# Parked S5 matrices loaded back transfer by transfer, small mixer weights split one stage earlier, and a margin before the step transposes, in a two-block fp32 kernel

## The chip, the cores and the metric

The kernel runs on 1 core of one Trainium2 chip. The metric is device microseconds of one execution, taken as the median of several runs. Engines are named as in the profile: PE is TensorE matmul, PEld its weight loads, DVE is VectorE, ACT is ScalarE, POOL is GpSimd, SP is SyncE, which computes nothing and issues the DMAs of one queue in program order.

## What is computed

The reference runs two blocks on 256 tokens of width 1024, in float32. The first is a hybrid attention block with a mixture of 32 experts. The second, which the change touches, is two layers of feed-forward, mixer, feed-forward:

```python
def second_block(x, ...):
    h = x
    for i in range(DEPTH_2):
        f = swiglu(rmsnorm(h, ffn1_pre_g[i]), ffn1_w_gate[i], ffn1_w_up[i], ffn1_w_down[i])
        h = h + 0.5 * rmsnorm(f, ffn1_post_g[i])
        m = mixer(rmsnorm(h, mix_pre_g[i]), w_in[i], ...)
        h = h + rmsnorm(m, mix_post_g[i])
        f = swiglu(rmsnorm(h, ffn2_pre_g[i]), ffn2_w_gate[i], ffn2_w_up[i], ffn2_w_down[i])
        h = h + 0.5 * rmsnorm(f, ffn2_post_g[i])
    return h

def mixer(u, ...):
    proj = u @ w_in
    z, xbc, dt_raw, u5, g_a, g_b = jnp.split(proj, SPLITS, axis=-1)
    y_a = ssd_branch(z, xbc, dt_raw, ...) @ w_branch_a
    y_b = s5_branch(u5, ...) @ w_branch_b
    return (jax.nn.sigmoid(g_a) * y_a + jax.nn.sigmoid(g_b) * y_b) @ w_out
```

`ssd_branch` needs the step `dt = softplus(dt_raw + bias)` and its running sums. `s5_branch` is a complex linear recurrence over 64 groups; the kernel runs it in blocks of time with matrices that depend on the weights alone.

## The kernel before

Products of float32 are made as three matmuls of two rounded halves (`mm3`: high by high, high by low, low by high). So each weight unit, 1 MB loaded by SP into one of three buffers (`raw`, `NRAW = 3`), is split in two halves of 1024 columns: ACT casts the high part (`whi`), POOL or DVE subtracts to get the low part (`wlo`), and PE uses both. Four halves exist at a time; a cast waits for PE to be done with the half four before, and a load waits for the second subtraction of the unit three before (`drop`, `load`). A half is 24 matmuls of 256 columns.

The order of instructions on every engine is written out at build time by a small planner. `Clocks` and `Engine` hold a planned time for each engine from a cost for each instruction; side work runs as generators (`Thread`), and `stir`, called after every six matmuls of a unit, takes the next step of each thread whose planned time `ready` has come (within `EARLY` = 0.7 us of PE's planned clock). A thread that yields a float waits so many planned us of PE's clock (`step`). The planner counts a 256-column matmul as 256 x 0.00042 = 0.1075 us and a 256 KB load as 0.73 us behind those before it (`spread`).

The feed-forward stage (`ffn`) streams 33 units: 22 of gate and up, 11 of down. The mixer starts with the boundary (normalization and the first product), four units `u` for the S5 input, the small product for the step (`dps`, 24 matmuls with the split weights `dw`), then the units of `PLAN`, eight of `z` first.

Three side works matter here. `s5_pre` computed the S5 matrices during the expert stage and parked them in DRAM (`ld`, `gd`, `kd`, `ed`). `s5_build` loads them back during a feed-forward stage: for layer 0 in the first one, for layer 1 in the second of layer 0; `mixer` finishes it before the first `z`. For each half it loads `LT` and `BT` (eight transfers of 256 KB that fill 64 rows each, written with a source whose outer dimension is 4) and `toep` (eight of 64 KB from `kd`), and multiplies `LT` and `BT` on DVE (`cmul`, six operations). Then it loads `G` and `E` (eight of 512 KB over 128 rows). The waits between are `GAP`. `ssd_steps` makes `dt` and the sums from `dps` and has PE transpose them. `small_weights` in the mixer scales the convolution weights `cw` and splits `dtw` into `dw`.

All work is recorded at L155, the helper of `Engine`, so rows are told apart by their tiles: `ffn_`, `bnd_`, `u_`, `z_`, `x_`, `dt_`, `s5b_` (build), `s5i_` (run), `ssd_`. `p` is a ring of working tiles.

Of the kernel before, what the change touches and what calls it, by code (L numbers as in the profile page):

```python
# [10 lines left out]
F32 = mybir.dt.float32  # L11
F32R = mybir.dt.float32r
# [3 lines left out]
P = 128  # L16
T = 256
KD = 8
# [3 lines left out]
def dram_ap(t, offset, dims):  # L22
    return bass.AP(tensor=t.tensor, offset=t.offset + offset, ap=[list(d) for d in dims])
# [155 lines left out]
class Core:  # L179
# [4 lines left out]
    KEEP = ("raw", "whi", "wlo", "ident", "causal", "ones_d", "ones_g", "eps", "one", "one32", "junk", "id16", "s5_r4", "vecs")  # L184
    MID = ("iota", "four", "group", "upper", "ones", "mod", "adaA", "rw", "rb")
    NRAW = 3
    GAP = 20.0, 10.0, 25.0, 12.0
    LENT = ()
    pages, stop = None, 1 << 30
    lab = "k"  # L190
# [62 lines left out]
    def vec(self, name):  # L253
        off, n = self.voff[name]
        return self.vecs[:, off:off + n]
# [186 lines left out]
    def step(self, th):  # L442
        c, lab = self.nc, self.lab
        n, c.end, self.stepping, self.lab = c.count, 0.0, True, th.lab
        th.step()
        th.lab, self.lab, self.stepping = self.lab, lab, False
        if c.count > n:
            th.ready = c.end
        if isinstance(th.wait, float):
            th.ready = c.tensor.clock + th.wait  # L450
        if th.done:
            self.threads.remove(th)
        return c.count > n or th.done
# [146 lines left out]
class Block2(Core):  # L600
# [219 lines left out]
    def s5_pre(self, l):  # L820
# [113 lines left out]
        for hf in range(2):  # L934
            self.lab = "s5b"
            G = t8([P, 2, H, 4, 16])
            pp = slice(hf * H, hf * H + H)
            cr, nci = G0[:, 0, pp], G0[:, 1, pp]
            tmp = t4([P, 2, 2, H, 16])
            for k in range(4):  # L940
# [66 lines left out]
    def s5_build(self, l, res):  # L1007

        nc, a = self.nc, self.a
        NP, H = 32, 16  # L1010
        made = self.s5_made[l]
        ld, kd = made["ld"], made["kd"]
        self.lab = "s5b"
        toep, win = [], []
        for hf in range(2):
            yield self.GAP[hf]
            yield from self.need(p4=8)
            self.lab = "s5b"
            tp = self.p4([P, H, 64])
            LT = self.p4([P, H, 64]), self.p4([P, H, 64])  # L1020
            BT = self.p4([P, H, 64]), self.p4([P, H, 64])
            for g in range(2):
                rows = slice(g * 64, g * 64 + 64)
                for ri in range(2):
                    nc.sync.dma_start(LT[ri][rows], dram_ap(ld, ((ri * 2 + g) * 4 * NP + hf * H) * 64, [[NP * 64, 4], [0, 16], [1, H * 64]]))
                    nc.sync.dma_start(BT[ri][rows], dram_ap(a["s5_bt"], (((l * 2 + ri) * 2 + g) * 16 * NP + hf * H) * 64,
                                                            [[0, 4], [NP * 64, 16], [1, H * 64]]))
                for j in range(4):
                    r0 = g * 64 + j * 16
                    nc.sync.dma_start(tp[r0:r0 + 16], dram_ap(kd, hf * H * 32 * 112 + g * 16 * 112 + (3 - j) * 16,  # L1030
                                                              [[112, 16], [32 * 112, H], [1, 64]]))
            yield self.GAP[2]
            self.lab = "s5b"
            wr, wi, tmp = (self.p4([P, H, 64]) for _ in range(3))
            for _ in self.cmul(wr, wi, LT[0], LT[1], BT[0], BT[1], wi, tmp):
                yield
            self.give(p4=3 if hf else 5)
            toep.append(tp)
            win.append((wr, wi))
        yield from self.need(p4=8)  # L1040
        self.lab = "s5b"
        G = [[self.p4([P, H, 4, 16]) for _ in range(2)] for _ in range(2)]
        E = [[self.p4([P, H, 64]) for _ in range(2)] for _ in range(2)]
        for hf in range(2):
            for ri in range(2):
                half = slice(ri * 1024, ri * 1024 + 1024)
                nc.sync.dma_start(E[hf][ri].rearrange("p h m -> p (h m)"), made["ed"][hf, :, half])
                nc.sync.dma_start(G[hf][ri].rearrange("p h k c -> p (h k c)"), made["gd"][hf, :, half])
            yield self.GAP[3]
        res.update(win=win, toep=toep, G=G, E=E, r4=made["r4"])  # L1050


# [139 lines left out]

    def ssd_steps(self, l, dps, r, res):

        nc, a, v = self.nc, self.a, self.v
        self.lab = "dt"
        hvt = self.t([32, 2], "hvt")
        nc.gpsimd.dma_start(hvt, a["hvec"][l])  # L1200
        y, e, u, w_, dt, adt, ac = (self.p1()[:32] for _ in range(7))
        v.tensor_mul(y, dps, r[:32])
        self.give(ps=1)
# [19 lines left out]
        for c in range(2):  # L1223
            cc = slice(c * P, c * P + P)
            v.tensor_tensor_scan(ac[:, cc], self.one32, adt[:, cc], 0.0, op0=ALU.mult, op1=ALU.add)
        yield 2
        yield from self.need(ps=1)
        self.lab = "dt"
        acd = self.scratch([32, T], "acd")
# [149 lines left out]

    def mixer(self, l, h, banks, build, s5):
        nc, a = self.nc, self.a
        v, q = self.v, self.q
        gpre = self.vec(f"mpre{l}")
        lead, xu, rstd = self.boundary(h, banks, self.vec(f"f1post{l}"), gpre, "u")
        self.lab = "u5"
        cw = self.t([P, 24, 5], "cw")
        nc.sync.dma_start(cw, a["conv2"][l])
        dtw = self.p1([P, KD, 32])  # L1390
        nc.sync.dma_start(dtw, a["wdt"][l])
        dw = self.p1([P, KD, 32], F32R), self.p1([P, KD, 32], F32R)
        ud = self.scratch([1024, T], "ud")

        def ev_u5(grp, ps):
# [30 lines left out]
        r = rstd()  # L1426
# [2 lines left out]
        sc = self.defer(scale)  # L1429
        self.budget = self.BM  # L1430

        def small_weights():
            v.tensor_scalar_mul(cw, cw, 0.5)
            nc.scalar.copy(dw[0], dtw)
            yield
            v.tensor_sub(dw[1], dtw, dw[0].bitcast(F32))
        for g in (2, 3):
            pg = self.bank()
            self.unit_mm(("u", g), xu, pg)
            self.defer(lambda g=g, pg=pg: ev_u5(g, pg))  # L1440
            if g == 2:
                sw = self.defer(small_weights)
        self.finish(sw)
        self.roomy, self.busy, self.seen = False, 0, 0
        dps = self.bank()[:32, :T]
        for k in range(KD):
# [2 lines left out]
        self.settle()  # L1449
        s5t = self.spawn(self.s5_run(s5, ud, s5))  # L1450
        sd = {}
        self.spawn(self.ssd_steps(l, dps, r, sd))
        self.finish(sc)
        xg, zg, gat = FM([None] * 6), FM([None] * 4), FM([None] * 4)

# [111 lines left out]
        for grp in range(8):  # L1567
            self.lab = "ba"
            ps = self.bank()
            for i in range(2):  # L1570
                w = [z.rearrange("p (k c) -> p k c", k=KD) for z in self.half(("ba", grp))]
# [35 lines left out]
    def block2(self, h, layers=2, first=None):  # L1607
        self.scale_gains(layers)
        banks, g = None, None
        s5, build = first or self.s5_start(0)  # L1610
        for l in range(layers):
            vec = lambda name: self.vec(f"{name}{l}")
            self.budget = self.BF if l else self.B0
            acc = self.ffn(l, h, banks, g, vec("f1pre"))
            acc = self.mixer(l, h, acc, build, s5)
            self.budget = self.BF
            if l + 1 < layers:
                s5, build = self.s5_start(l + 1)
            banks, g = self.ffn(l, h, acc, vec("mpost"), vec("f2pre")), vec("f2post")
        self.close(h, banks, g)  # L1620
# [1376 lines left out]
```

## Time and profile before

| | us |
|---|---|
| median of 3 runs | 3071.73 (3071.64 to 3073.94) |
| the profiled execution | 3076.65 |
| its span, first to last instruction | 3074.4 |
| PE busy | 2668.1 (87%) |
| DVE busy | 1689.6 (55%) |
| POOL busy | 1442.4 (47%) |
| mean granted clock of PE | 0.95 |

The profiled execution took 4.9 us more than the median. Of its time the first block takes about 1279 us, then come, by the first PE work of each stage: feed-forward 1 of layer 0 (1279 to 1517), its mixer (to 1975), feed-forward 2 (to 2210), feed-forward 1 of layer 1 (to 2410), its mixer (to 2871) and feed-forward 2 (to the end). A row of the trace gives a start and a length in us, or for a group the busy time; brackets hold the idle time of that engine before it and what ended it. A granted clock of 1.00 is 2.4 GHz and 0.50 is 1.2 GHz. Rows of the DMA give the share of 16 DMA engines that was busy and the rate.

### The profile page before, as it was taken

How to read it: one execution, taken by the hardware profiler on the slowest of the kernel's cores; microseconds unless marked ns; L12 is line 12 of the kernel's file. 1: busy time of each engine (PE TensorE's matmuls, PEld its weight loads, DVE VectorE, ACT ScalarE, POOL GpSimd, SP SyncE). 2: the span in 40 equal slices, each digit the busy share in tenths (PEclk: the TensorE clock that was granted, in tenths of full speed). 3: DMA queues.
4: the chain of work that ended last, by engine and by line, in shares of the span. 5: the costliest groups of instructions: out<-in, count | busy, mean ns of one | idle time of the engine just before them, and what ended most of it. 6: DMA issues, size and time to landing. Idle time of an engine off the chain costs nothing.

```text
span 3074.4 us, 55096 instructions
## 1 busy us (share of the span) xinstructions
PE 2668.1 (87%) x22727; PEld 2062.3 (67%) x22727; DVE 1689.6 (55%) x2657; ACT 1020.0 (33%) x1516; POOL 1442.4 (47%) x733
## 2 busy tenths in 40 slices
PE   5768988889889888877989888977999889998998
PEld 4655333333333333577979888977999889888998
DVE  8995242333433211355577888655554685886644
ACT  4562100001000000233445554433444445544444
POOL 7651000000000000256756666756788657766786
PEclk9778999999999999998999999988999999999999
DMA  7526999999999999655545434455555445444453
GB/s 285 191 86 262 420 420 394 420 420 417 418 419 417 414 421 420 255 171 185 195 144 168 157 138 140 162 171 185 192 181 190 157 122 179 151 151 138 162 185 120
DMA packets 146540, 755.09 MB, mean 246 GB/s; under 512 B 47264, under 2 KB 51824, under 8 KB 59760
## 3 DMA queue, kind: packets, MB, share of 16 engines
q1 hardware_dynamic: 140672, 729.30, 62.6%
q0 software_dynamic: 5472, 21.71, 1.9%
q8 instruction: 183, 3.00, 0.4%
q14 instruction: 69, 0.57, 0.1%
q10 hardware_dynamic: 144, 0.52, 0.0%
HBM read 736.50 MB, written 14.97 MB: 244 GB/s over the span
## 4 chain that ended last, share of the span: by engine, by line
PE 36%; DVE 10%; issue 4%; DMA 3%; ACT 2%; POOL 2%; SPq 1%; ACTq 0%; DVEq 0%; POOLq 0%
PE ffn_ps L155 18%; PE x_ps L155 3%; PE ba_ps L155 3%; DVE ssd_p L155 3%; PE g_ps L155 2%; DMA s5b_p<-s_bt 2%; PE glu_ps L155 2%; PE bnd_ps L155 2%; PE z_ps L155 2%; POOL ffn_wlo L155 2%; PE wo_ps L155 1%; DVE x_p L155 1%; PE ssd_ps L155 1%; DVE u_p L155 1%; SPq L155 1%
## 5 line engine op out<-in xcount | busy, mean ns | idle before, releaser
L155 POOL TENSOR_TENSOR ffn_wlo<-ffn_raw,ffn_whi 128x1024 fp32r<-128x1024 f32 x227 | 569.9, 2537 | 178.4 <-ACT ffn_whi L155 172.7
L155 PE MATMUL ffn_ps<-bnd_p,ffn_whi 128*128 128x256 f32 x2560 | 469.2, 285 | 28.8 <-ACT ffn_whi L155 28.8
L155 PEld LDWEIGHTS ffn_ps<-bnd_p,ffn_whi 128*128 128x128 f32 x2560 | 404.5, 194 | 29.6 <-ACT ffn_whi L155 29.6
L155 PE MATMUL ffn_ps<-bnd_p,ffn_wlo 128*128 128x256 f32 x1280 | 366.4, 286 | 13.7 <-POOL ffn_wlo L155 13.7
L155 ACT CAST ffn_whi<-ffn_raw 128x1024 fp32r<-128x1024 f32 x232 | 240.3, 1046 | 259.4 <-PE ffn_ps L155 174.0
L155 PE MATMUL down_ps<-up_place,tr_p 128*32 128x512 f32 (+1 forms) x2048 | 244.0, 614 | 82.1 <-DMA up_place<-edn 82.1
L155 DVE TENSOR_TENSOR ffn_p<-ffn_p,ffn_p 128x256 f32<-128x256 f32 (+1 forms) x184 | 260.9, 1420 | 91.8 <-ACT ffn_p L155 91.4
L155 PE MATMUL ffn_ps<-ffn_p,ffn_whi 128*128 128x256 f32 x1408 | 258.9, 286 | 29.5 <-ACT ffn_whi L155 28.1
L155 PEld LDWEIGHTS ffn_ps<-bnd_p,ffn_wlo 128*128 128x128 f32 x1280 | 248.8, 194 | 15.9 <-POOL ffn_wlo L155 15.9
L155 PE MATMUL up_ps<-down_place,prep_p 128*32 128x512 f32 (+1 forms) x1920 | 224.8, 596 | 21.4 <-DMA down_place<-eup 21.3
L155 PEld LDWEIGHTS ffn_ps<-ffn_p,ffn_whi 128*128 128x128 f32 x1408 | 222.5, 194 | 30.1 <-ACT ffn_whi L155 28.5
L155 PE MATMUL up_ps<-up_place,prep_p 128*32 128x512 f32 (+1 forms) x2048 | 230.2, 595 | 8.3 <-DMA up_place<-eup 8.2
L155 PEld LDWEIGHTS down_ps<-up_place,tr_p 128*32 128x32 f32 x2048 | 67.8, 112 | 244.6 <-issue 200.5
L155 DVE TENSOR_SCALAR glu_p<-up_ps 128x512 f32<-128x512 f32 x64 | 44.1, 691 | 311.7 <-PE up_ps L155 311.7
L155 PE MATMUL ffn_ps<-ffn_p,ffn_wlo 128*128 128x256 f32 x704 | 201.0, 286 | 0.9 <-DVE ffn_wlo L155 0.9
L155 DVE TENSOR_TENSOR ffn_p<-ffn_ps,ffn_p 128x512 f32<-128x512 f32 x80 | 55.1, 689 | 208.6 <-PE ffn_ps L155 208.4
L155 PEld LDWEIGHTS up_ps<-up_place,prep_p 128*32 128x32 f32 x2048 | 61.8, 109 | 150.3 <-issue 129.1
L155 DVE COPY scat_p<-down_ps 128x512 f32<-128x512 f32 x16 | 11.1, 691 | 245.7 <-PE down_ps L155 245.7
L155 PEld LDWEIGHTS up_ps<-down_place,prep_p 128*32 128x32 f32 x1920 | 57.3, 109 | 129.2 <-issue 125.5
L155 PEld LDWEIGHTS ffn_ps<-ffn_p,ffn_wlo 128*128 128x128 f32 x704 | 136.7, 194 | 1.5 <-DVE ffn_wlo L155 1.5
L155 POOL DMA_DIRECT2D ed<-s5b_raw x4 | 2.1, 538 | 262.8 <-DVE s5b_raw L155 262.8
L155 POOL TENSOR_TENSOR scat_wlo<-scat_raw,scat_whi 128x1024 fp32r<-128x1024 f32 x2 | 4.7, 2364 | 251.1 <-ACT scat_whi L155 251.1
(832 smaller groups left out, 6547.7 us busy)
## 6 DMA issues: line engine op xcount, KB each, us to landing
up_place<-eup SPq DMA_DIRECT2D x128, 1024.0 KB, 10.9
up_place<-edn SPq DMA_DIRECT2D x128, 1024.0 KB, 13.7
down_place<-eup SPq DMA_DIRECT2D x120, 1024.0 KB, 14.1
ffn_raw<-gu SPq DMA_DIRECT2D x75, 1024.0 KB, 5.0
ffn_raw<-dn SPq DMA_DIRECT2D x40, 1024.0 KB, 4.9
x_raw<-win SPq DMA_DIRECT2D x22, 1024.0 KB, 5.0
z_raw<-win SPq DMA_DIRECT2D x16, 1024.0 KB, 4.9
g_raw<-win SPq DMA_DIRECT2D x10, 1024.0 KB, 5.4
```

Source lines behind the costliest of these rows:

```text
L155: return f(out, *args, **kw)
```

## The change

- `s5_build` no longer issues the loads of a half in one go. It waits `GAP[0]` = 8 planned us, then issues one `LT` and one `BT` at a time with `GAP[1]` = 5 after each pair, four pairs to a half; after the fourth `GAP[2]` = 8 and the multiplication on DVE. The same for the second half. Then `E` (four loads, 5 after each), `toep` (sixteen, `GAP[3]` = 4 after each) and `G` (four, 5 after each). It asks for 7, 7, 4 and 8 tiles of the ring instead of 8, 8 and 8.
- `mixer_small` is a new thread that starts with the feed-forward 1 of each layer. It loads `cw`, `hvt` and `dtw` by SP, waits 40 planned us, and scales and splits them, into tiles of their own. The mixer no longer loads or splits them, and `ssd_steps` no longer loads `hvt` by POOL.
- A thread may yield a negative float: it is then ready that many planned us after its own last operation ends or after PE's planned clock, whichever is later. `ssd_steps` yields -6.0 in place of 2 before the transposes.

```diff
-    GAP = 20.0, 10.0, 25.0, 12.0
+    GAP = 8.0, 5.0, 8.0, 4.0
...
-            th.ready = c.tensor.clock + th.wait
+            th.ready = c.tensor.clock + th.wait if th.wait > 0 else max(c.end, c.tensor.clock) - th.wait
...
+        yield self.GAP[0]
         for hf in range(2):
-            yield self.GAP[hf]
-            yield from self.need(p4=8)
-            self.lab = "s5b"
-            tp = self.p4([P, H, 64])
+            yield from self.need(p4=7)
             LT = self.p4([P, H, 64]), self.p4([P, H, 64])
             BT = self.p4([P, H, 64]), self.p4([P, H, 64])
             for g in range(2):
                 rows = slice(g * 64, g * 64 + 64)
                 for ri in range(2):
+                    self.lab = "s5b"
                     nc.sync.dma_start(LT[ri][rows], dram_ap(ld, ((ri * 2 + g) * 4 * NP + hf * H) * 64, [[NP * 64, 4], [0, 16], [1, H * 64]]))
                     nc.sync.dma_start(BT[ri][rows], dram_ap(a["s5_bt"], (((l * 2 + ri) * 2 + g) * 16 * NP + hf * H) * 64,
                                                             [[0, 4], [NP * 64, 16], [1, H * 64]]))
-                for j in range(4):
-                    r0 = g * 64 + j * 16
-                    nc.sync.dma_start(tp[r0:r0 + 16], dram_ap(kd, hf * H * 32 * 112 + g * 16 * 112 + (3 - j) * 16,
-                                                              [[112, 16], [32 * 112, H], [1, 64]]))
+                    yield self.GAP[1]
             yield self.GAP[2]
...
-        yield from self.need(p4=8)
+        yield from self.need(p4=4)
         self.lab = "s5b"
-        G = [[self.p4([P, H, 4, 16]) for _ in range(2)] for _ in range(2)]
         E = [[self.p4([P, H, 64]) for _ in range(2)] for _ in range(2)]
         for hf in range(2):
             for ri in range(2):
...
+                nc.sync.dma_start(E[hf][ri].rearrange("p h m -> p (h m)"), made["ed"][hf, :, ri * 1024:ri * 1024 + 1024])
+                yield self.GAP[1]
+        yield from self.need(p4=8)
+        self.lab = "s5b"
+        toep = [self.p4([P, H, 64]) for _ in range(2)]
+        for hf in range(2):
+            for g in range(2):
+                for j in range(4):
...
+                    nc.sync.dma_start(toep[hf][r0:r0 + 16], dram_ap(kd, hf * H * 32 * 112 + g * 16 * 112 + (3 - j) * 16,
+                                                                    [[112, 16], [32 * 112, H], [1, 64]]))
+                    yield self.GAP[3]
...
+                nc.sync.dma_start(G[hf][ri].rearrange("p h k c -> p (h k c)"), made["gd"][hf, :, ri * 1024:ri * 1024 + 1024])
+                yield self.GAP[1]
...
-        hvt = self.t([32, 2], "hvt")
-        nc.gpsimd.dma_start(hvt, a["hvec"][l])
...
-        yield 2
+        yield -6.0
         yield from self.need(ps=1)
...
+    def mixer_small(self, l):
+
+        nc, a = self.nc, self.a
+        self.lab = "msm"
+        cw, hvt, dtw = self.t([P, 24, 5], "cw"), self.t([32, 2], "hvt"), self.t([P, KD, 32], "dtw")
+        dw = self.t([P, KD, 32], "dwh", dt=F32R), self.t([P, KD, 32], "dwl", dt=F32R)
+        for t, w in ((cw, "conv2"), (hvt, "hvec"), (dtw, "wdt")):
+            nc.sync.dma_start(t, a[w][l])
+        self.small = cw, dw, hvt
+        yield 40.0
+        self.lab = "msm"
+        self.v.tensor_scalar_mul(cw, cw, 0.5)
+        nc.scalar.copy(dw[0], dtw)
+        yield
+        self.v.tensor_sub(dw[1], dtw, dw[0].bitcast(F32))
...
+            self.early = self.spawn(self.mixer_small(l))
             acc = self.ffn(l, h, banks, g, vec("f1pre"))
```

## Rows read from the trace of the kernel before

**Rows 1.** Stages: length; busy PE, PEld, DVE, ACT, POOL; PEclk, DMA share, GB/s
```profile
1279.00:1516.80 237.80, 200.75 (x1587) 198.51 (x1587) 124.14 (x100) 92.65 (x130) 158.19 (x67) 0.92 0.54 182
1975.50:2209.20 233.70, 196.72 (x1571) 194.30 (x1572) 128.88 (x107) 91.16 (x127) 158.76 (x67) 0.92 0.53 182
2220.00:2410.20 190.20, 189.20 (x1572) 188.81 (x1572) 95.03 (x92) 91.84 (x127) 160.00 (x70) 1.00 0.50 172
1516.80:1975.50 458.70, 411.41 (x3742) 396.96 (x3742) 348.54 (x490) 217.92 (x297) 307.60 (x147) 0.95 0.46 152
```

**Rows 2.** Waits of PE, 1275 to 1525: us in total, times, longest
```profile
PE ffn_ps L155 <- ACT ffn_whi L155: 28.2, 3, 14.4
...
PE ffn_ps L155 <- POOL ffn_wlo L155: 6.3, 4, 1.9
```

**Rows 3.** Timeline of SP's queue, 1270 to 1530: start, length, instruction
```profile
1320.57 0.69 SPq L155 DMA_DIRECT2D s5b_p<-ld  x1
...
1339.12 5.65 SPq L155 DMA_DIRECT2D s5b_p<-kd  x4
1344.89 2.48 SPq L155 DMA_DIRECT2D ffn_raw<-dn  x1
```

**Rows 4.** DMA issues, KB each, median us to landing: 1319.9-1339, 1338.8-1352, 2220-2410.2
```profile
s5b_p<-kd SPq DMA_DIRECT2D x4, 64.0 KB, 15.3
...
s5b_p<-kd SPq DMA_DIRECT2D x4, 64.0 KB, 12.4
...
ffn_raw<-gu SPq DMA_DIRECT2D x18, 1024.0 KB, 5.0
```

**Rows 5.** Short stretches of the first batch, columns as in rows 1
```profile
1342.00:1346.00 4.00, 0.00 (x0) 0.00 (x0) 0.00 (x0) 0.00 (x0) 0.00 (x0) 1.00 0.33 112
...
1350.00:1354.00 4.00, 0.00 (x0) 0.00 (x0) 0.00 (x0) 0.00 (x0) 0.00 (x0) 0.50 1.00 357
```

**Rows 6.** Timelines of SP, ACT, POOL, 2278 to 2300, no parked loads
```profile
2280.50 6.86 SPq L155 DMA_DIRECT2D ffn_raw<-gu  x2
...
2292.63 1.04 ACT L155 CAST ffn_whi<-ffn_raw 128x1024 fp32r<-128x1024 f32 x1
...
2293.75 7.52 POOL L155 TENSOR_TENSOR ffn_wlo<-ffn_raw,ffn_whi 128x1024 fp32r<-128x1024 f32 x3 [1.75 <-ACT ffn_whi L155]
```

**Rows 7.** A stretch at the lower clock, columns as in rows 1
```profile
1383.80:1390.40 6.60, 4.68 (x23) 4.68 (x23) 3.46 (x2) 3.01 (x5) 6.60 (x3) 0.50 0.18 35
```

**Rows 8.** Waits of PE in the mixer of layer 0, 1517 to 1975
```profile
PE dt_ps L155 <- DVE dt_p L155: 7.9, 2, 4.2
...
PE u_ps L155 <- DVE u_p L155: 4.7, 1, 4.7
...
PE u_ps L155 <- ACT u_p L155: 1.6, 1, 1.6
```

**Rows 9.** Chain that ended last, 1545 to 1605: start, length, what
```profile
1557.45 4.42 PE u_ps L155 x22
...
1599.40 3.56 PE z_ps L155 x18
```

**Rows 10.** Timeline of DVE, 1551 to 1600: start, length, instruction
```profile
1552.55 1.61 DVE L155 TENSOR_SCALAR u_cw<-u_cw 128x120 f32<-128x120 f32 x1
1554.08 2.58 DVE L155 TENSOR_TENSOR u_p<-u_p,u_p 128x256 fp32r<-128x256 f32 x1
...
1558.05 0.97 DVE L155 TENSOR_TENSOR u_p<-u_p,u_p 128x256 fp32r<-128x256 f32 x2
...
1567.72 0.67 DVE L155 TENSOR_SCALAR dt_p<-dt_p,dt_hvt 32x256 f32<-32x256 f32 x1 [5.40 <-DMA dt_hvt<-hvec]
1577.39 0.75 DVE L155 TENSOR_TENSOR s5i_p<-s5i_ps,s5b_p 128x256 f32<-128x256 f32 x2 [9.00 <-PE s5i_ps L155]
```

**Rows 11.** Timeline of POOL, 1550 to 1566
```profile
1554.03 2.35 POOL L155 TENSOR_TENSOR u_wlo<-u_raw,u_whi 128x1024 fp32r<-128x1024 f32 x1
```

**Rows 12.** A stretch of the mixer, columns as in rows 1
```profile
1580.00:1600.00 20.00, 12.12 (x139) 11.35 (x139) 19.69 (x28) 7.05 (x9) 10.18 (x6) 0.88 0.24 82
```

More of the change, by code (lines that the diff above doesn't have):

```diff
@@ L1036, in s5_build @@
                 yield
-            self.give(p4=3 if hf else 5)
-            toep.append(tp)
+            self.give(p4=5)
             win.append((wr, wi))
-        yield from self.need(p4=8)
+        yield from self.need(p4=4)
         self.lab = "s5b"
-        G = [[self.p4([P, H, 4, 16]) for _ in range(2)] for _ in range(2)]
         E = [[self.p4([P, H, 64]) for _ in range(2)] for _ in range(2)]
@@ L1045, in s5_build @@
             for ri in range(2):
[L1046 to L1049, printed above, removed]
+                self.lab = "s5b"
+                nc.sync.dma_start(E[hf][ri].rearrange("p h m -> p (h m)"), made["ed"][hf, :, ri * 1024:ri * 1024 + 1024])
+                yield self.GAP[1]
+        yield from self.need(p4=8)
+        self.lab = "s5b"
+        toep = [self.p4([P, H, 64]) for _ in range(2)]
+        for hf in range(2):
+            for g in range(2):
+                for j in range(4):
+                    self.lab = "s5b"
+                    r0 = g * 64 + j * 16
+                    nc.sync.dma_start(toep[hf][r0:r0 + 16], dram_ap(kd, hf * H * 32 * 112 + g * 16 * 112 + (3 - j) * 16,
+                                                                    [[112, 16], [32 * 112, H], [1, 64]]))
+                    yield self.GAP[3]
+        self.lab = "s5b"
+        G = [[self.p4([P, H, 4, 16]) for _ in range(2)] for _ in range(2)]
+        for hf in range(2):
+            for ri in range(2):
+                self.lab = "s5b"
+                nc.sync.dma_start(G[hf][ri].rearrange("p h k c -> p (h k c)"), made["gd"][hf, :, ri * 1024:ri * 1024 + 1024])
+                yield self.GAP[1]
         res.update(win=win, toep=toep, G=G, E=E, r4=made["r4"])
@@ L1191, in s5_run, with ssd_steps @@
         self.give(p4=2)
-    def ssd_steps(self, l, dps, r, res):
+    def ssd_steps(self, hvt, dps, r, res):
         nc, a, v = self.nc, self.a, self.v
         self.lab = "dt"
-        hvt = self.t([32, 2], "hvt")
-        nc.gpsimd.dma_start(hvt, a["hvec"][l])
         y, e, u, w_, dt, adt, ac = (self.p1()[:32] for _ in range(7))
@@ L1387, in mixer @@
         self.lab = "u5"
[L1388 to L1392, printed above, removed]
+        self.finish(self.early)
+        cw, dw, hvt = self.small
         ud = self.scratch([1024, T], "ud")
@@ L1430, in mixer @@
         self.budget = self.BM
[L1432 to L1436, printed above, removed]
         for g in (2, 3):
@@ L1440, in mixer @@
             self.defer(lambda g=g, pg=pg: ev_u5(g, pg))
-            if g == 2:
-                sw = self.defer(small_weights)
-        self.finish(sw)
         self.roomy, self.busy, self.seen = False, 0, 0
@@ L1451, in mixer @@
         sd = {}
-        self.spawn(self.ssd_steps(l, dps, r, sd))
+        self.spawn(self.ssd_steps(hvt, dps, r, sd))
         self.finish(sc)
```

## The prediction, made before the changed kernel ran

> **What bounds the kernel now.** I read the busy time by stage first. Three feed-forward stages do the same matmuls; the one in which nothing is loaded back takes 190.2 us with PE at full clock, the two in which `s5_build` runs take 237.8 and 233.7 at a mean clock of 0.92 [rows 1]. So the two builds cost about 44 us each (the first stage also opens at the lower clock; I leave its other 4 out). The clean stage gives the unit of all that follows: 190.2 us / 1572 matmuls = 0.121 us, so a half is 2.9 us and a unit 5.8 us. POOL's three subtractions in 7.52 us [rows 6] make 5.0 us a unit, so POOL catches up only 0.8 us per unit.
>
> Second, the waits of PE in the first of the two stages: 28.2 us for casts and 6.3 us for low parts [rows 2]. Third, SP's queue and the DMA at that place. The first transfer of a batch goes out at 1320.57; the next weight load is issued only at 1344.89, behind the batch [rows 3]. In between the DMA engines are 33% busy at 112 GB/s, while plain weight loads fill them: share 1.00 at 357 GB/s [rows 5]. A third of 16 is about five: the `LT` and `BT` transfers use few engines and queue up there. So bandwidth is not short; a few engines are, and SP's queue holds the weights back. Fourth, the mixer: PE waits 7.9 us for the step transposes and 4.7 + 1.6 us for the split weights of the step product [rows 8].
>
> **Paced loads: the terms.** The landings price a transfer. A batch of eight 256 KB transfers and eight `kd` begins at 1320.57; its last `kd` loads, issued from 1339.12 on, land 12.4 us later, at about 1351.8 [rows 3, 4]. Less the 5.0 us that a load takes when nothing is ahead of it [rows 4], that is 26.2 us, 3.3 a transfer at most. By bytes (2.1 MB of 2.6) it is 2.6. I take 3.0, so a pair costs its engines 6.0 us (5.2 to 6.6). A weight load takes 0.50 of a unit's 5.8 us, 2.9 us, of every engine [rows 1], these too.
>
> The new pace is 5 planned us. The planner steps a thread up to 0.7 us early and looks every six matmuls (0.645 planned), so a pair comes every 4.5 planned us, 5.1 real, against a unit of 5.8 real: about one pair per unit. The few engines then have 6.0 + 2.9 = 8.9 us of work per 5.8: every pair makes the following weights 3.1 us later (2.3 to 3.7). Eight pairs: 25 us (18 to 30).
>
> Against that stands a reserve. In the clean stage a unit issued at 2280.50 lands 5.0 us later [rows 4, 6] and is cast at 2292.63: 7.1 us spare. The cast is about three halves ahead of use (8.7 us), and the first subtraction ends 3.6 us after the cast begins [rows 6]: 5.1 us spare. Together 12 us. Between the two halves (8 planned us and a multiplication of some 7) three units pass and give back about 2. So 25 - 14 = 11 us of stall remain (4 to 16, and up to 22 if the reserve is not yet full where the first pairs come, 12 planned us earlier than now). After a stall PE runs slower: between 1383.80 and 1390.40 its clock is 0.50, that is 1.2 GHz, after short waits, and the 4.7 us busy there would have been 2.3 [rows 7]. One or two such stretches: 3 us (0 to 8). **A build stage keeps 14 us of its 44 (4 to 30): gain 30, twice 60** (28 to 80).
>
> What rows show about the engines is only their number. The Trainium skill ("DMA: Bandwidth & Descriptors", "Why a DMA increments its semaphore by 16 and not by 1") says that a transfer uses the largest number up to 16 that divides the slowest dimension on both sides, and SP's transfers the lowest-numbered engines: 4 here, always the same. The share of 0.33 agrees, with some other traffic in it. By that rule pacing cannot spread this load, and the residue of 14 stays. But the same page ("Rules for kernel authors") says that transfers to one half of the partitions spray over all 16 engines; by that, a pair would be gone in little over a microsecond, which is rival B.
>
> The other paced loads: `E` and `G` are 512 KB over 128 rows, half of 2.9 us of every engine; with 2.9 for weights this stays under 5.8, so nothing. `toep` is 64 KB each and waits mostly behind others now [rows 4]; nothing, and up to 0.5 us each if SP's issue of them delays weights. SP issues the same number of transfers as before. All of them take 8 + 14.5 + 14 + 14.5 + 15 + 18 + 62 + 18 planned us, about 165, or 185 real, which fits a stage of 190 plus four `u` units; what is left at `z` would be a few `G` at 1.5 us.
>
> The new wait on DVE: `cmul` is written 8 planned us (9 real) after the fourth pair, which lands some 18 us after its issue (12 of delay, 6 own). DVE then sits up to 9 us, and behind it the activation steps (`ffn_p`), which `down` needs three units (17 us) later: nothing; without that cover, 9 us a half.
>
> **Small weights.** PE stands 1.6 + 4.7 us for `dw`, then runs the 22 matmuls in 4.42 us instead of 2.7 [rows 8, 9]. Without that wait the product could begin at 1550.8 and end at 1553.7, but `z` needs the low parts of `xs`. DVE writes the last at about 1559.0 [rows 10], one 0.41 us subtraction of `dw` earlier in the new order: 1558.6. The first half of `z` then ends at about 1558.7 against 1561.87 + 2.9 = 1564.8 now: 6 us (5 to 7.7). The 7.7 would hold if the 1.61 us scaling of `cw` also came off.
> I do not count it: the subtraction behind it started at 1554.08, took 2.58, and ended when POOL's 2.35 us subtraction begun at 1554.03 did [rows 10, 11]; started sooner, it or the next would meet that one.
> The skill ("SBUF — State Buffer", "SBUF: two separate sides") names the cause: DVE with two SBUF inputs and POOL lock one port pair for a whole instruction. By it 6 us hold, without it 7.7.
>
> The moved work costs 1.6 + 0.4 us of DVE and 0.4 of ACT in a stage where DVE is busy 95 of 190 us [rows 1]: nothing, and 2.4 us if it fell on the activation steps. Its three loads lie at the head of a stage ahead of weights with 7 us spare: nothing. In the mixer DVE no longer waits 5.40 us for `hvt` [rows 10].
>
> **The margin.** PE reached the transposes about 8.5 us before `z` went on at 1599.40, 7.9 of it waiting, and the 18 matmuls after took 3.56 instead of 2.2 [rows 8, 9]. The margin of 6 planned us is 6.7 real. The 1.8 missing are covered by the 5.40 and by an earlier start of the chain, into 9.00 us in which DVE now idles [rows 10]. So 7.9 + 1.4 = 9 us (0 if PE runs ahead of DVE by as much as it gains; 9).
>
> Sum 15 us a mixer. Behind it DVE is busy 19.7 of 20 us [rows 12], so part returns as later waits for DVE; I take **12 a mixer, twice 24** (10 to 34).
>
> **Sum.** 60 + 24 = 84. On the profiled execution: 3076.65 - 84 = 2992.65. That one stands 4.9 above the median; stalls do not depend on it, so the median goes from 3071.73 to **2988**.
>
> **The rivals.** B, *the pace hides all*: transfers spread over all engines, or the reserve is larger. Both builds at the clean stage's time: 88 + 24 = 112, 2960. For it: the DMA as a whole is half idle. Against: 112 GB/s with eight transfers queued.
> C, *the change does less than it says*: threads are also stepped out of time, wherever the planner waits for room or for another thread (`rounds`), so pairs go out in bunches. A bunch of four pairs costs what it does now in one half: half of each 44 stays, 22 + 5 more clock: gain 2 x 17 + 24 = 58, 3014.
> D, *slower*: many short waits in place of two long ones, each bringing the lower clock. The paced stretch is some 170 us of PE's work; at half clock for a share s of it PE loses 170 s. It decides at 170 s = 44 + 12, s = a third. At s = 0.4: 68 a stage, 2 x 24 lost, 24 won back: 3096. For it: a wait of 4 us in all brought 6.6 us at 0.50 [rows 7]. Against: a slow PE lets the weights catch up, and the mixer with its 47 us of waits has a clock of 0.95 [rows 1].
>
> **How the numbers follow.** Forecast 0.55 (2988, own range 2968 to 3005), B 0.20, C 0.14, D 0.06; 0.05 for builds that gain nothing net. The range takes in B and C: 2955 to 3020. About 0.2% (6 us) can be told from no change: faster 0.90, same 0.03, slower 0.07.
>
> **What would show it.** Build stages of about 204 us with weights that land 8 to 17 us after issue behind pairs, PE waits of 2 to 4 us rather than 14, and two or three short stretches at 0.50. No wait for `dt`, no `hvt`, `z` begun 6 us sooner after the last `u`. It is wrong if weight loads land in 5 us behind pairs (B), if several pairs stand side by side in SP's queue (C), or if a build stage's mean clock falls under 0.8 (D).

## The result, and the profile of the changed kernel

The changed kernel takes 3019.46 us (median of four, 3014.19 to 3022.48) against 3072.74 (four, 3071.64 to 3073.94) for the kernel before: ratio 0.9825, 95% interval 0.9808 to 0.9842, 53 us less. The forecast was 2988 us, range 2955 to 3020: faster, as said, but by 53 us where 84 were expected. The time lies outside the forecast's own range (2968 to 3005) and half a microsecond inside the whole one, at the end that rival C had set.

I cut both profiled executions at four kinds of events that every kernel here has: the first `ffn_ps` matmul of a feed-forward stage, the first `u_ps`, the first `z_ps`, the first `wo_ps`. The second column holds the second build stage and the clean stage behind it. All in us, from the trace:

```
kernel               ffn to u   u to z  z to wo   ffn to u   u to z  z to wo
                     (layer 0)                    (build + clean)
before                  245.6     22.7    381.1      445.5     22.7    383.5
changed                 225.4     14.3    385.2      428.0     14.3    384.8
e1 paced loads only     218.9     21.8    384.0      430.7     22.1    381.2
e2 mixer edits only     245.5     14.3    385.4      445.3     14.3    384.5
e7 no margin            224.4     14.3    388.8      427.8     14.3    388.3
e8 changed, again       224.1     14.3    385.1      424.0     14.3    385.2
e12 wider pace          216.6     14.3    385.7      417.3     14.3    385.2
e3 loads split          211.5     14.3    385.0      413.7     14.3    385.4
e5 split, cmul spaced   207.1     14.3    385.4      406.9     14.3    385.3
e11 and `late` on POOL  207.5     14.3    377.6      404.2     14.3    381.6
```

So the builds gave 20.2 + 17.5 = 37.7 us (60 forecast) and the mixers, from `u` to `wo`, 4.3 + 7.1 = 11.4 (24 forecast). The other 4.8 of the 54 us between the two profiled executions lie ahead of the first stage, where nothing is changed; that point wanders between 1288.7 and 1294.5 in the kernels shown here, so those 4.8 us count as chance.

Windows that answer to [rows 1] (the second has 10 matmuls more than there, the third 81 fewer), with its columns (length; busy PE, PEld, DVE, ACT, POOL with their counts; PEclk, DMA share, GB/s), changed kernel: the two build stages and the clean one, then a stretch of the first mixer.

```profile
1274.30:1492.70 218.40, 203.23 (x1587) 200.55 (x1588) 112.69 (x100) 92.86 (x131) 158.80 (x69) 0.95 0.62 195
1944.90:2162.20 217.30, 201.28 (x1581) 198.16 (x1582) 116.89 (x108) 91.59 (x128) 160.80 (x70) 0.96 0.60 193
2184.00:2363.50 179.50, 178.77 (x1491) 178.60 (x1489) 88.40 (x75) 84.35 (x115) 154.33 (x65) 1.00 0.54 186
...
1541.00:1612.00 71.00, 61.13 (x821) 57.82 (x820) 68.48 (x93) 30.28 (x36) 37.33 (x23) 0.93 0.39 118
```

The clean stage is what it was (179.5 / 1491 = 0.120 us a matmul). The builds still take 218.4 and 217.3 us against 190.2 clean: 24 (with the 4 of the opening taken off) and 26 us (with the ten matmuls taken off) of their 44 are left, where I forecast 14. The clock is at 0.95 where I expected about 1. The last row matters for the mixer: DVE is busy 68.5 of 71 us.

The waits of PE in the first build stage (us in all, times, longest), which answer to [rows 2]:

```profile
PE ffn_ps L155 <- POOL ffn_wlo L155: 9.5, 7, 2.1
PE ffn_ps L155 <- ACT ffn_whi L155: 3.6, 3, 1.4
```

Seven waits of 34.5 us in all, three of them for casts and up to 14.4 us long, have become ten of 2.1 at most: 13.1 us, near the 11 forecast. Behind each group of them the clock falls to its lower level (0.50, 1.2 GHz), as in [rows 7]; columns as above:

```profile
1334.40:1341.20 6.80, 5.61 (x26) 5.61 (x27) 2.79 (x3) 0.38 (x1) 3.47 (x2) 0.50 0.52 186
1354.90:1358.30 3.40, 3.40 (x18) 3.40 (x17) 2.06 (x1) 2.12 (x3) 3.40 (x2) 0.50 0.41 117
1389.00:1392.40 3.40, 3.40 (x19) 3.40 (x18) 3.37 (x2) 0.00 (x0) 2.77 (x1) 0.50 0.08 34
1399.30:1402.70 3.40, 3.40 (x18) 3.40 (x17) 1.71 (x1) 1.83 (x3) 3.40 (x2) 0.50 0.29 63
```

Four stretches and 17 us, in the second build stage five and again 17, where one or two were forecast.

Next, why weights are still late. SP's queue and the chain that ended last (start, length, what), the place that answers to [rows 3]:

```profile
1315.46 0.54 SPq L155 DMA_DIRECT2D s5b_p<-ld  x1
1316.05 0.54 SPq L155 DMA_DIRECT2D s5b_p<-s_bt  x1
1320.19 0.33 SPq L155 DMA_DIRECT2D ffn_raw<-dn  x1
```

```profile
1320.19 20.53 DMA ffn_raw<-dn
...
1344.31 3.38 POOL ffn_wlo L155
1347.69 4.33 issue
...
1352.05 2.37 POOL ffn_wlo L155
```

The last pair of the first half leaves SP at 1315.46, the weights behind it at 1320.19, and from then until ACT casts them 20.5 us pass, where a load with nothing ahead takes 5.0 [rows 4]. The trace keeps the landings of a transfer part by part, and they show what held it: of the sixteen parts of the load issued at 1320.19, twelve have landed 7.0 us after issue, and the last four 19.6 to 20.5 us after. An `LT` or `BT` transfer has only four parts that land late, so the pairs run on four of the sixteen engines, and the weights behind them wait for those four. From one such landing to the next a pair takes the four 6.3 to 8.2 us and a weight load 2.4 to 2.7, where the prediction had 6.0 (5.2 to 6.6) and 2.9. The second half of the chain is another matter: between 1347.69 and 1352.05 nothing is in flight for it, and ACT stands. Timelines of DVE and ACT there (start, length, instruction, in brackets the idle time ahead of it and what ended it):

```profile
1338.34 10.43 DVE L155 TENSOR_TENSOR s5b_p<-s5b_p,s5b_p 128x1024 f32<-128x1024 f32 x5 [7.75 <-DMA s5b_p<-s_bt]
1348.69 0.68 DVE L155 TENSOR_TENSOR ffn_p<-ffn_ps,ffn_p 128x512 f32<-128x512 f32 x1
...
1349.41 0.42 ACT L155 ACTIVATE ffn_p<-ffn_p 128x256 f32<-128x256 f32 x1 [6.59 <-DVE ffn_p L155]
...
1350.93 1.99 ACT L155 CAST ffn_whi<-ffn_raw 128x1024 fp32r<-128x1024 f32 x2
```

DVE waits 7.75 us in the multiplication for the last pair (forecast: up to 9), then computes until 1348.69, and only then the step `ffn_p`. ACT's activation waits for that step at the head of ACT's queue, 6.59 us, and the two casts of the next weights stand behind it, their data there since 1343.2. I had written that nobody misses `ffn_p` for 17 us; `down` doesn't, but the casts behind it in ACT's queue do.

The waits of PE from `z` to `wo` in the first mixer, which answer to [rows 8]:

```profile
PE z_ps L155 <- POOL z_wlo L155: 6.9, 1, 6.9
...
PE dt_ps L155 <- DVE dt_p L155: 3.0, 1, 3.0
PE z_ps L155 <- DVE u_p L155: 2.0, 1, 2.0
```

The waits for the split step weights are gone, the one for the step transposes went from 7.9 to 3.0 us, and a wait of 6.9 us for low parts of `z` is new. POOL's timeline shows what those stand behind, a memset that waits 8.06 us for DVE:

```profile
1594.02 0.15 POOL L155 MEMSET s5b_p<- 128x8 f32 x2 [8.06 <-DVE s5i_p L155]
1594.11 7.65 POOL L155 TENSOR_TENSOR z_wlo<-z_raw,z_whi 128x1024 fp32r<-128x1024 f32 x3
```

### The profile page after: what moved, and what is told of

It is laid out like the page before. It is cut to its first block, busy times and chain, and to the rows that moved or that the text cites. A ratio compares the mean times of both kernels' runs of the same rounds, so it can differ in the third digit from the quotient of the medians.

```text
span 3020.7 us, 55114 instructions
## 1 busy us (share of the span) xinstructions
PE 2669.7 (88%) x22727; PEld 2065.7 (68%) x22727; DVE 1651.5 (55%) x2663; ACT 1022.0 (34%) x1518; POOL 1416.7 (47%) x725
## 4 chain that ended last, share of the span: by engine, by line
PE 34%; DVE 12%; issue 4%; POOL 3%; ACT 2%; DMA 2%; ACTq 0%; POOLq 0%; DVEq 0%
PE ffn_ps L155 20%; PE x_ps L155 4%; DVE ssd_p L155 3%; PE ba_ps L155 3%; DVE x_p L155 2%; POOL ffn_wlo L155 2%; PE bnd_ps L155 2%; DMA ffn_raw<-dn 2%; PE wo_ps L155 2%; PE g_ps L155 1%; DVE xbc_p L155 1%; DVE u_p L155 1%; DVE bnd_p L155 1%; PE s5o_ps L155 1%; POOL z_wlo L155 1%
## 5 line engine op out<-in xcount | busy, mean ns | idle before, releaser
L155 DVE TENSOR_TENSOR ffn_p<-ffn_p,ffn_p 128x256 f32<-128x256 f32 (+1 forms) x184 | 250.7, 1365 | 103.6 <-ACT ffn_p L155 103.3
```

What stands on the lines that cost most here:

```text
L155: return f(out, *args, **kw)
```

## The experiments

**e1 and e2: the parts by themselves.** e1 is the kernel before with the new `s5_build` and its GAP; e2 is the changed kernel with the old ones.

> The kernel before with the new `s5_build` and its GAP alone; small weights and step transposes as before. If the two parts add, it keeps what the two build stages gained between the two profiles (19.4 and 17.9 us): about 3035 us. If the new order of loads hurts the mixer that follows (the last `G` now land while `z` runs) and the other edits only made up for that, the mixers come out longer than before and it stands at 3040 to 3050. If the gain of the build stages came from the moved small weights, it stands near 3073.

> The kernel before with `mixer_small` and the margin of 6 alone; `s5_build` and its GAP as before. If the two parts add, the mixers keep the 5 and 7 us that they gained between the profiles: 3058 to 3062 us. If the prediction's price of the mixer was right (12 each) and it is the new load order that takes half of it back, 3048. If these edits give nothing, 3073.

e1: 3034.04 us against 3070.36, ratio 0.9882 (0.9865 to 0.9898), 36 us. e2: 3063.36 against the same, 0.9974 (0.9964 to 0.9984), 7 us. They move different stages, as the table shows: e1 the two with builds, e2 only `u` and what follows. e1's two mixers together are no longer than before, so no cost of the late `G` loads shows in their sum. In the stages of the table the parts bring 42 and 12 us, the changed kernel 49 and, profiled again (e8), 54; by the medians it is 43 against 51 to 53, with intervals of 3 to 7 us on each side. So the parts may well add up, and nothing can be said of the difference.

**e8: the changed kernel once more**, beside other kernels.

> The changed kernel once more, unaltered, beside the three others. The parts alone gave 36 and 7 us, the whole 53: if they add, the whole is 40 to 46 us under the kernel before; if the whole brings more than its parts, 50 to 56.

3018.25 us against 3069.62, 0.9835 (0.9814 to 0.9856): 51 us, the second of the two, though the interval (44 to 57 us) does not exclude the first.

**e3: the same loads on more engines.** Each `LT` and `BT` load of 64 rows becomes four of 16 rows. The order in which everything else is issued stays, instruction by instruction. The edit in short:

```
-  nc.sync.dma_start(LT[ri][rows], dram_ap(ld, ..., [[NP * 64, 4], [0, 16], [1, H * 64]]))
+  for j in range(4):
+      nc.sync.dma_start(LT[ri][g * 64 + j * 16:g * 64 + j * 16 + 16], dram_ap(ld, ..., [[0, 16], [1, H * 64]]))
...
```

> The changed kernel with each LT and BT load of 64 rows issued as four loads of 16 rows; the planned order of all other work is the same. Theory: a 64-row load uses a few engines only, and the weights queue behind it there; 16 rows spread over all engines, so a pair is gone in about 1.5 us, `ffn_raw` lands 5 to 8 us after issue behind a pair, the short PE waits (13 us a stage) and most of the half-clock stretches (8 to 9 us) go: 20 to 25 us a stage, 2970 to 2980 us. Rival: SP's order or POOL's low parts set the pace of the waits, not the number of engines: 3010 to 3025, and later by a few us for the 96 more issues on SP.

2999.44 us against 3070.36, 0.9768 (0.9751 to 0.9784): 19 us below the changed kernel, half of what I expected. The first build stage, from `ffn` to `u`, columns as above:

```profile
1293.70:1505.20 211.50, 201.72 (x1642) 199.49 (x1641) 132.90 (x120) 96.39 (x134) 170.56 (x74) 0.98 0.62 207
```

The DMA issues of its paced stretch, 1288 to 1400 (count, KB each, median us to landing):

```profile
ffn_raw<-gu SPq DMA_DIRECT2D x12, 1024.0 KB, 5.3
ffn_raw<-dn SPq DMA_DIRECT2D x5, 1024.0 KB, 5.1
```

Timelines of SP at one pair, and of DVE, ACT and POOL at the multiplication behind it:

```profile
1301.59 0.33 SPq L155 DMA_DIRECT2D ffn_raw<-gu  x1
1301.96 1.88 SPq L1019 DMA_DIRECT2D s5b_p<-ld  x4
1303.88 4.30 SPq L1019 DMA_DIRECT2D s5b_p<-s_bt  x4
1308.29 0.37 SPq L155 DMA_DIRECT2D ffn_raw<-dn  x1
...
1330.38 15.87 DVE L155 TENSOR_TENSOR s5b_p<-s5b_p,s5b_p 128x1024 f32<-128x1024 f32 x6
...
1346.89 0.42 ACT L155 ACTIVATE ffn_p<-ffn_p 128x256 f32<-128x256 f32 x1 [10.04 <-DVE ffn_p L155]
...
1327.59 15.19 POOL L155 TENSOR_TENSOR ffn_wlo<-ffn_raw,ffn_whi 128x1024 fp32r<-128x1024 f32 x5
1349.53 4.89 POOL L155 TENSOR_TENSOR ffn_wlo<-ffn_raw,ffn_whi 128x1024 fp32r<-128x1024 f32 x2 [6.75 <-ACT ffn_whi L155]
```

Weights now land in 5.1 to 5.3 us at the median and 7.1 at most, instead of up to 22, with the same bytes in the same order; each parked transfer now lands in sixteen parts, not four. The late weights came from the few engines, as the prediction had it. That agrees with the Trainium skill ("DMA: Bandwidth & Descriptors", "Why a DMA increments its semaphore by 16 and not by 1"): a slowest dimension of 4 gives 4 engines, one of 16 all of them. What is left is the other chain. The six operations of the multiplication take 15.87 us on DVE, and ACT's gap at `ffn_p` has grown to 10.04 us; POOL runs dry for 6.75 us behind it, and PE waits 2.2 and 1.6 us. So a good part of what the earlier weights bring is given back here: with weights on time POOL subtracts without a pause, and four of the six operations take 3.3 to 3.4 us (the two after POOL had run dry 1.2).

**e4: the same split without the pacing.** The edit of e3 in the kernel before.

> The kernel before with the same split, its loads still in bunches of eight. Theory of the few engines: a batch of 2.1 MB then takes about 6 us of all engines, which the 12 us of reserve cover beside the `kd` loads; most of the 44 us a stage goes without any pacing: 2990 to 3015 us. Rival, that the bunching itself (the queue on SP, 24 us from the first load of a batch to the next weight load) is what costs: 3060 to 3075.

3045.82 us against 3070.36, 0.9922 (0.9905 to 0.9938): 25 us, between the two expectations. SP's queue through one batch:

```profile
1317.47 1.94 SPq L1019 DMA_DIRECT2D s5b_p<-ld  x4
...
1336.50 1.89 SPq L155 DMA_DIRECT2D s5b_p<-kd  x4
1338.50 0.39 SPq L155 DMA_DIRECT2D ffn_raw<-dn  x1
```

The 40 transfers of a batch now go out in 21 us, 0.46 us each with a pause or two, and the weights behind them are issued only then, 21 us after the batch began. Spread transfers alone bring 25 us, against 36 for the pace alone (e1) and 71 for both with the mixer's edits (e3), because SP still hands out all of them ahead of a weight load; pacing and spreading remove two different queues, SP's and that of the few engines.

**e12: the pace alone, wider.** Pairs 10 planned us apart instead of 5, loads of 64 rows as they are.

```
-  GAP = 8.0, 5.0, 8.0, 4.0
+  GAP = 8.0, 5.0, 8.0, 1.5, 10.0
...
-                    yield self.GAP[1]
-            yield self.GAP[2]
+                    yield self.GAP[4]
+            yield self.GAP[2]
```

> The changed kernel with 10 planned us between the pairs of LT and BT instead of 5 (the other gaps of `E` and `G` stay at 5, `toep` goes out 1.5 apart to make up for it); loads of 64 rows, the multiplication as it is. The pairs then go out one behind every second weight load. By the prediction's price (a pair 6.0 us and a weight 2.9 us of the few engines, a unit of 5.8 us) that is 11.8 us of work in 11.6: the weight behind a pair lands some 6 us late and nothing piles up, so the waits for late weights go as in the split version and only the multiplication on DVE stays: 2998 to 3006 us. If the split helped by something else than the queue on a few engines, or if a pair costs much more than 6 us, it stays at 3012 to 3022.

3004.53 us against 3071.02, 0.9781 (0.9765 to 0.9798): in the range that follows from the price, though not all of its reason holds. The weights behind the four pairs of the first half land 10.4, 10.2, 15.5 and 14.3 us after issue, so with pairs 11 to 12 us apart the few engines still fall behind a little; the reserve covers most of it (PE waits 8.7 us in the first stage, where it waited 13.1). With a pair for each weight load they fall behind by more. The edit also moved the `toep` loads closer and so changed the planned order; that part of it was not tried by itself.

**e5: the multiplication spread out**, on e3.

```
-  for _ in self.cmul(wr, wi, LT[0], LT[1], BT[0], BT[1], wi, tmp):
-      yield
+  for op, o, x, y in ((self.v.tensor_mul, wi, LT[0], BT[0]), (self.v.tensor_mul, tmp, LT[1], BT[1]), ...):
+      op(o, x, y)
+      yield self.GAP[4]
...
-  GAP = 8.0, 5.0, 8.0, 4.0
+  GAP = 8.0, 5.0, 8.0, 1.5, 5.0
```

> The split version (loads of 16 rows), with the six operations of the multiplication in `s5_build` given out one by one, 5 planned us apart, instead of in pairs one behind the other; `toep` loads 1.5 instead of 4 apart to make up for it. In the split version weights land in 5 to 6 us, and yet PE waits 2 to 4 us once per half: DVE is 16 us in the multiplication, the activation step `ffn_p` waits for DVE at the head of ACT's queue (gap of 10.0 us), and the casts of the weights stand behind it. If that is the rest of the loss, ACT's gaps shrink to 4 us, the PE waits go, and each build stage loses 6 to 9 us more: 2980 to 2988 us. If the waits come from POOL or from the loads, or DVE is simply full there, nothing or 5 us at most: 2994 to 3002.

2987.81 us against 3069.62, 0.9731 (0.9710 to 0.9751): 12 us below e3. Both build stages, columns as above; a timeline of ACT; waits of PE in the first stage:

```profile
1290.90:1498.00 207.10, 200.81 (x1642) 198.95 (x1641) 142.85 (x119) 96.35 (x134) 174.59 (x74) 0.99 0.64 211
1940.80:2150.00 209.20, 204.42 (x1672) 202.51 (x1671) 143.97 (x119) 97.12 (x133) 179.62 (x75) 0.99 0.64 211
```

```profile
1346.12 0.42 ACT L155 ACTIVATE ffn_p<-ffn_p 128x256 f32<-128x256 f32 x1 [6.33 <-DVE ffn_p L155]
```

```profile
PE ffn_ps L155 <- POOL ffn_wlo L155: 2.6, 4, 1.4
```

The gap shrank to 6.33 us only (I expected 4), yet no wait for `ffn_whi` is left and 2.6 us for low parts. Against this row the changed kernel's own stage divides: it is 225.4 us with PE busy for 208.3, so it is idle for 17.1 and not 6.3, 10.8 us more, and busy for 7.5 us more with the same matmuls, which is the lower clock.

**e9: the spacing without the split.** The edit of e5 on the changed kernel.

> The changed kernel with the multiplication of `s5_build` given out one operation at a time (5 planned us apart, `toep` 1.5 apart), its LT and BT loads of 64 rows as they are. The split alone brought 19 us, the multiplication on top of it 12. If the two losses lie side by side and add, this one shows 3006 us (2 x 6 under 3018). If the late loads hold the multiplication and the casts anyway, the spacing brings nothing without the split: 3015 to 3022.

3027.32 us against 3070.43, 0.9857 (0.9840 to 0.9873): 9 us above the changed kernel, which neither theory said. SP and ACT in the second half show that this run is not the test I meant:

```profile
1382.56 0.54 SPq L155 DMA_DIRECT2D s5b_p<-ld  x1
...
1383.72 0.51 SPq L155 DMA_DIRECT2D s5b_p<-ld  x1
...
1387.11 2.13 SPq L155 DMA_DIRECT2D ffn_raw<-dn  x1
...
1410.30 1.99 ACT L155 CAST ffn_whi<-ffn_raw 128x1024 fp32r<-128x1024 f32 x2 [14.54 <-DMA ffn_raw<-dn]
```

The planner's new order put two pairs side by side; the weights behind them were cast 23 us after their issue, and PE waited 6.6 us at once. It shows the price of a bunch (the prediction's rival C), which the changed kernel pays too, at 1970.00 and 1971.23 in its second build stage. What the spacing brings without the split stays open.

**e7: the changed kernel without the margin.**

```
-        yield -6.0
+        yield 2
```

> The changed kernel with `yield 2` instead of the margin of 6 before the step transposes. If the margin is worth the 9 us a mixer of the prediction: 3034 to 3038 us. If the small weights alone bring what the mixers gained (5 to 7 each) and the margin only moves the wait to the low parts of `z` behind POOL: 3017 to 3024.

3030.08 us against 3069.62, 0.9873 (0.9856 to 0.9889): 12 us above e8. Its `z` to `wo` parts are 3.7 and 3.1 us longer, which is what the margin is worth, not 9; of the rest, 3.8 us lie in the second build and the clean stage, whose code this edit doesn't touch. In it PE waits 6.1 us in all for the transposes, and DVE, behind PE, 7.07 us for the first `s5i_ps`; PE's waits from `z` to `wo`, and a timeline of DVE:

```profile
PE dt_ps L155 <- DVE dt_p L155: 6.1, 2, 5.5
```

```profile
1557.18 0.76 DVE L155 TENSOR_TENSOR s5i_p<-s5i_ps,s5b_p 128x256 f32<-128x256 f32 x2 [7.07 <-PE s5i_ps L155]
```

**e6: the memsets off POOL's queue.**

```
-                q.memset(zr[:, :, 0:1], 0.0)
-                q.memset(zi[:, :, 0:1], 0.0)
+                v.memset(zr[:, :, 0:1], 0.0)
+                v.memset(zi[:, :, 0:1], 0.0)
```

> The changed kernel with the two small memsets after each scan in `s5_run` on DVE instead of POOL, and nothing else. In the changed kernel POOL stands 8 us at such a memset, for DVE's last read of `zr` and `zi`, with the low parts of the `z` weights queued behind it, and PE waits 6.9 and 6.7 us for those in the two mixers. If that queue is where the gain of the mixer went, both waits go and 10 to 13 us come back: 3004 to 3010 us. If PE then only waits later for DVE (the step scan, `ssd`), it stays at 3014 to 3022.

3023.45 us against 3069.62, 0.9851 (0.9829 to 0.9873): no gain. The wait for `z_wlo` is gone, and one of the same size has come for DVE's output (waits of PE from `z` to `wo`):

```profile
PE s5o_ps L155 <- DVE s5b_p L155: 7.3, 2, 6.7
```

So POOL's queue was where PE met the delay, not its cause. That is DVE, busy almost without a break (68.5 of 71 us) from the step product to the end of the scans.

**e10 and e11: work taken off DVE**, on e5: the subtractions after the scans left out, or computed by POOL (the edit shown is e11's).

```
             if late:
-                v.tensor_sub(*late)
+                q.tensor_sub(*late)
...
```

> The version of e5 with one subtraction of 504 elements after each of the four scans of `s5_run` left out (`late`): that part of the rotation is not computed, which takes 8 x 0.94 = 7.5 us a mixer off DVE. Theory: in the first 70 us after the start of `z` DVE is busy without a break and sets when `s5o` can start, so the `z` to `wo` part of each mixer loses 5 to 7 us: 2974 to 2978 us. Rival: the mixer's length is set later, by `xbc` and the state-space groups, or by PE itself, and these 70 us are slack: 2984 to 2989.

> The version of e5 with the same subtractions computed by POOL instead of DVE. If DVE is the bound and POOL has the time, it gets most of what leaving them out gives: 2975 to 2983 us. If POOL's order (it stands 3 to 8 us at waits for DVE in that stretch, with the low parts of weights behind it) makes the chain of scans longer, it is no better or worse than e5: 2986 to 3000.

e10: 2977.25 us against 3070.43, 0.9693 (0.9677 to 0.9709). e11: 2974.77 against the same, 0.9686 (0.9670 to 0.9702): 13 us below e5, and the fastest of all kernels here, 44 us below the changed kernel with the whole computation in it. `z` to `wo` is 7.8 us shorter in the first mixer (6.9 in e10) and 3.7 (1.9) in the second. What was taken off DVE is not the 7.5 us a mixer of my expectation: the trace of e5 has four such subtractions in a mixer, not eight, of 0.68 us each or 2.8 to 2.9 where one meets a subtraction of POOL, 4.9 us in the first mixer and 7.1 in the second. So e10 came out in its range with a gain of 6.9 and 1.9 us, not of 5 to 7 in each mixer, and gain and work taken off do not go one to one. The 71 us of e11 that answer to the last row of the first fence, and, from its waits of PE from `z` to `wo`, what is left of POOL's:

```profile
1528.00:1599.00 71.00, 66.35 (x887) 62.84 (x887) 66.00 (x89) 30.18 (x37) 43.35 (x28) 0.95 0.40 118
```

```profile
PE g_ps L155 <- POOL z_wlo L155: 1.7, 2, 1.2
```

PE does 887 matmuls in them instead of 821. Why the second mixer gives less, for more work taken off, no run told.

## Why the prediction was right, and where it was wrong

**The bound, and the price of a transfer: right.** A few engines held the weights back; the landings show four, e3 takes the queue away by the shape of the transfers, e12 most of it by the pace, and both find a gain. A pair and a weight load were to take 8.9 us of these engines and took 8.7 to 10.7. That the time lies inside the range is in part luck: the range was drawn wide for the rivals, and 4.8 us of the difference between the profiled executions are not the change's. Rival B fell with the 20.53 us of the changed kernel's chain, and with it, for transfers of this shape, the other rule of the Trainium skill ("DMA: Bandwidth & Descriptors", "Rules for kernel authors"), that transfers to one half of the partitions spray over all engines: by e3 it is the shape that counts.

**The stall: size right, one cause missed.** 13.1 us of waits in the first stage and 14.9 in the second, against 11. But part of them were not late weights. The step that failed reads "DVE then sits up to 9 us, and behind it the activation steps (`ffn_p`), which `down` needs three units (17 us) later: nothing". The 9 us came (7.75, and 7.7 to 9.8 in the other halves). Priced at nothing because of the last reader of `ffn_p`, they reach PE by another way, for ACT waits for the same step with the casts queued behind it: 6.6 us of ACT's time, 3.3 and 3.2 of PE's in the first stage, and in e3, without any late weight, 3.8 and 1.9. e5 takes 12 us off by giving the multiplication out in pieces (and the `toep` loads closer together).

**The lower clock: the term mis-sized.** "One or two such stretches: 3 us (0 to 8)". There were four and five, 17 us each time, and they cost 10 us a stage by PE's busy time for the same matmuls: 208.3 and 209.0 us, where the clean stage takes 198.4 and e11, whose build stages have no such stretch, 198.8. The rows, cut at the events of the table (columns as above): clean stage and first build stage before, both build stages of the changed kernel, the second of e11.

```profile
2230.70:2431.70 201.00, 198.42 (x1643) 197.29 (x1642) 103.38 (x105) 95.14 (x131) 167.09 (x75) 1.00 0.51 174
1293.50:1539.10 245.60, 206.96 (x1643) 204.15 (x1642) 134.75 (x120) 95.83 (x133) 165.44 (x72) 0.92 0.53 181
...
1288.70:1514.10 225.40, 208.34 (x1642) 204.77 (x1641) 123.68 (x120) 96.01 (x134) 166.44 (x74) 0.96 0.61 194
1957.00:2184.00 227.00, 209.04 (x1643) 205.39 (x1642) 122.84 (x117) 94.31 (x131) 167.43 (x74) 0.96 0.60 194
...
1936.40:2139.60 203.20, 198.80 (x1642) 197.27 (x1641) 138.59 (x116) 94.64 (x131) 177.15 (x74) 1.00 0.66 216
```

The row I had taken it from [rows 7] showed that waits of 4 us in all bring a stretch; ten short waits spread over 72 us brought four in the first stage. In the kernel before the first stage was busy for 207.0 us, so the change took 21.6 us of idle time and none of the loss to the clock. That was rival D's mechanism, at a share of a tenth (17 of some 170 us), where it decides at a third.

**`u` and the small weights: right.** The prediction took its 6 us (5 to 7.7) where the first half of `z` ends. From the first `u_ps` to the 24th `z_ps`, the last of that half, it is 25.5 and 25.9 us before and 19.7 in both mixers of the changed kernel: 5.7 and 6.2. The 8.4 of the table are the first `z_ps`; PE then waits 2.0 us for the low parts that the prediction named (`z_ps <- DVE u_p`).

**The margin and what comes back: both mis-sized.** 3.7 and 3.1 us for the margin, where the prediction took 9 from the wait itself; as I read it, PE's wait for the transposes and DVE's for `s5i_ps` behind it overlap, and removing them brings what DVE gains, not what PE waited. And without the margin only 0.7 and 3.6 us of the 5.7 and 6.2 are left at `wo` (e7 against the kernel before), so 5.0 and 2.6 are lost again behind `z`, where 3 were taken off for both edits. The row for it was there, DVE at 19.7 of 20 us [rows 12], and I used it for a discount when it was the bound of the whole stretch: DVE is busy for 68.5 of 71 us there, e6 shows that PE waits for its end by whatever way, and e10 that less of it is a shorter mixer, by 6.9 us in the first and 1.9 in the second.

**The sum.** 60 - 37.7 in the builds is 22 too much. By the rows above, the first build stage of the changed kernel is 24.4 us longer than the clean one: PE is idle for 14.5 us more and busy for 9.9 more, where the prediction had 11 and 3. Against e11's, the nearest to a clean one with the same ends, the second is 23.8 longer, 13.6 idle and 10.2 busy. So 14 of the 22 us are the clock and 6 the waits. The last 2 lie in the price of 44: cut at these events, the second build stage of the kernel before (1986.2 to 2230.7, 244.5 us) is 41 longer than e11's, not 44; my clean window [rows 1] began 10 us after the stage did. 24 - 11.4 is 13 in the mixers, the margin and what is lost behind `z`. 84 - 22 - 13 is 49, and the 4.8 us ahead of the first stage make up the 54 between the profiled executions. The time came out near rival C's 3014, but C is not the main reason: pairs stand side by side in the second stage only, and at one place.

## What to carry to other kernels

A wait on an in-order engine is to be costed through all that is queued behind it on that engine and on those that wait for it at the head of their own queue, not by the last reader of its result. Where a trace shows an engine busy without a break between two points, that stretch is a bound: an earlier start pays only as far as this engine's work begins sooner or gets less. Short waits spread out cost more than their length where they bring the lower clock, so take the PE's busy time of the same matmuls before and after as well as its waits.

## What the runs showed of the hardware that I had not expected

- DVE and POOL together: a multiplication of 128x1024 f32 takes 1.23 us on DVE alone and 3.3 to 3.4 us beside POOL's subtractions, which go from 2.4 or 2.6 to 3.38 us at the same time. The Trainium skill ("SBUF — State Buffer", "SBUF: two separate sides") has the two take turns at one port pair, a whole instruction each; the equal 3.4 us of both nearly agree (1.23 and 2.4 in turn are 3.6). I had applied that rule in the mixer and not in the build, where it doubles the multiplication from 7.4 us (six at 1.23) to 15.87.
- SP spends 0.42 to 0.46 us on a transfer of 64 KB and 0.54 on one of 256 KB, so the split multiplies its time per byte by more than three; a batch of 40 then holds SP for 21 us, and the weights wait for it (e4).
- In e3 the eighth parked transfer of a pair is issued at 1307.88, just as the weight load issued ahead of the pair has landed (1307.86), and so at every pair: eight in flight, and the next waits. In the trace SP's DMAs count on eight semaphores in turn, and the ninth waits for the one that it takes over. So it is the program that sets this limit here; whether the chip has one no run told.
